# The order of the weight-part products, half-size weight buffers and side-by-side gate products in a two-layer decoder kernel

## The chip, the cores and the metric

The kernel runs on one core of one Trainium2 chip. The metric is the device time of one execution, in microseconds (us), taken as the median of several runs. Lower is better.

## The reference, cut to what matters

A small decoder with two layers works on 272 tokens (16 learned "meta" tokens and 256 input tokens) of width 2048, with 16 heads of 128.

```python
h = concat([meta, x])                        # 272 x 2048
# layer 0: attention with forget gates
a = rms_norm(h, norm_attn[0])
q, k, v, f_logit = split(a @ fox_w_in)       # 3 x 2048 columns, and 16 of f_logit
cum_logf = cumsum(log_sigmoid(f_logit + b_f))
h = h + forgetting_attention(q, k, v, cum_logf) @ fox_w_o
h = h + square(relu(rms_norm(h, norm_mlp[0]) @ w_up[0])) @ w_down[0]      # D_FF = 8192
# layer 1: stick-breaking attention over one shared K/V
k, v = split(rms_norm(h, kv_norm) @ w_kv)
q = rms_norm(h, norm_attn[1]) @ sb_w_q
h = h + stick_breaking_attention(q, k, v) @ sb_w_o
h = h + square(relu(rms_norm(h, norm_mlp[1]) @ w_up[1])) @ w_down[1]
return rms_norm(h, final_norm)[16:]          # the meta tokens are dropped
```

All is float32. Nearly the whole of the arithmetic is in the products with the weight matrices.

## The kernel before, in words

**Layout.** Activations lie feature-major: `hT` has 128 partitions, 16 chunks of features and 272 tokens. Layer 1 needs the meta tokens only for keys and values, so its queries, output projection and MLP run on 256 tokens; layer 0 and the keys and values of layer 1 run on 272.

**Split products.** A float32 product is made of products of the faster type `float32r`. Each weight block is split into a high part `whi` (ScalarE copies it into float32r, L205) and a low part `wlo` (VectorE subtracts the high part from the weights, L206). The activations are split in the same way, into `hi` and `lo`, which lie side by side in one tile (`both`). The product is high by high, high by low and low by high. In layer 0 these are three products of 272 columns (L228, L229, L230). In layer 1 the first two are one product of 512 columns, `whi` with `both` (L225), and the third is a product of 256 columns, `wlo` with `hi` (L226). Such a couple is called a pair. The two halves of a layer 1 bank are added when the bank is evacuated (`total`, L238 to L243: a ScalarE copy, a VectorE add).

**Groups.** `gemm_group` (L169 to L232) computes 512 output columns over all 2048 features. It runs four blocks `kb` of 512 features; a block has four chunks `kc` of 128. The 512 columns are four slices `m` of 128, each with a PSUM bank of its own (`acc`; the pool `pacc` has four banks, so the next group takes over the banks of this one as they are evacuated). A group thus has 64 (`kc`, `m`) steps: 192 products in layer 0, 64 pairs in layer 1. There are 96 groups in order: 12 of layer 0's queries, keys and values (Q, K, V for each of four sets of heads), 4 of its output projection, 32 of its MLP (four times 4 up and 4 down), then 4 of layer 1's queries, 8 of its keys and values, 4 of its output projection and 32 of its MLP.

**Weights.** One block is 1 MB, loaded by SyncE into a buffer `raw` (pool `wraw`, three buffers, L38) by one DMA (L193). Each half of a block (two chunks) is split into one `whi` and one `wlo` (pool `wspl`, three of each, L41). In the first group the DMAs are finer, 1, 2, 2 and 4 chunks by block, and `load_x` (L251) loads and splits the input between them.

**Order.** Inside a block the products are written half by half, and in each half bank by bank with two chunks each (L212); in the last block bank by bank with all four chunks (L216); in the first block of the first group chunk by chunk (L214). This written order isn't the one that runs: the program is built by a scheduler that simulates the engines in time and gives each engine a queue of its own; it may move a product past another whose data it expects later. At run time every engine works through its queue in order, and semaphores hold an instruction back until its data is there.

**Norms.** RMS norms are applied after the products: a group multiplies with the weights first, and the evacuation multiplies by `rstd`. `Norm.add` (L141) sums squares by chunk; `Norm.finish` (L150) makes a product with a matrix of 1/2048 (L153) into a bank `pms` of the pool `patt` and then a chain on VectorE and ScalarE. In the first up group of an MLP, `get_rstd` (L460) is called ahead of block 3; so is `get_rstd1` (L501) in the first query group of layer 1 (L514).

**Gates.** Group 1 is the first query group. Behind it come the gates (L281): 48 products of 272 columns with 16-column weights (L286, L287, L288), a VectorE multiplication by `rstd`, the bias, a logarithm of the sigmoid (ScalarE and VectorE), a cumulative sum over tokens (a scan on VectorE, L299), two transposes, and a trip through DRAM that spreads the sums over the partitions (`fk`, L358). The keys' group follows, and `decays` (L361, L364) are VectorE instructions behind the weight splits of its blocks.

**Start.** Seven products of a constant with itself (`idle`, L59 and L60) run on TensorE before the first data is there.

## Time and profile before

| | |
|---|---|
| Median of 3 runs | 2354.8 us (2354.66 to 2355.55) |
| The profiled run | 2355.27 us |
| Its span, first to last instruction | 2353.6 us |
| TensorE busy (PE) | 2339.7 us, 99% |
| VectorE busy (DVE) | 1343.7 us, 57% |
| ScalarE busy (ACT) | 1056.2 us, 45% |
| GpSimd busy (POOL) | 33.4 us, 1% |
| Weights and all else moved by DMA | 411.92 MB, 175 GB/s in the mean |
| Granted TensorE clock, mean over the span | 0.998 of full |

How to read it: one execution is recorded by the hardware's profiler. PE is TensorE's row of products, PEld its row of weight loads, which run beside the products. A product's recorded length holds its way through the array, and the next one starts before it ends; so what counts for the throughput is the distance from one start to the next, and not the length. "L225" is line 225 of the kernel. In a timeline, "x4" is four like instructions in a row, with the time from the first start to the last end. "[0.94 <-DVE ssq_a L148]" says that the engine stood idle for 0.94 us ahead of this instruction, and what it waited for. In a table of windows each row is a stretch of time, its length, and then for PE, PEld, DVE, ACT and POOL the busy time and the number of instructions, followed by the granted TensorE clock, the share of the DMA engines in use and GB/s. In a list of the costliest groups the columns are the busy time, the mean length in ns of one, and the idle time ahead of them with its releaser.

### The profile page before, as it was taken

The page shows a single profiled execution, that of the slowest core. Times are in us where ns is not written, and L with a number is a line of the kernel's source. Part 1 is how long each engine was busy: PE and PEld are TensorE (multiplying, and loading weights), DVE is VectorE, ACT ScalarE, POOL GpSimd, SP SyncE. Part 2 cuts the span into 40 slices and gives each one's busy share as a digit, 9 for nine tenths or more (in the row PEclk, how much of TensorE's full clock was granted, in tenths as well). Part 3 has the DMA queues.
Part 4 walks back from the last instruction along what each step waited for, and adds up shares of the span by engine and source line. Part 5 has one row for each costly group of instructions (what it writes and reads, how often), then busy time and mean ns, then how long its engine had stood idle before and what let it go on. Part 6 is the DMA issues. An engine that isn't in the chain of part 4 may idle for free.

```text
span 2353.6 us, 39103 instructions
## 1 busy us (share of the span) xinstructions
PE 2339.7 (99%) x16496; PEld 2207.5 (94%) x16496; DVE 1343.7 (57%) x1920; ACT 1056.2 (45%) x1471; POOL 33.4 (1%) x58
## 2 busy tenths in 40 slices
PE   9999999999999999999999999999999999999998
PEld 9999999999999999999998999988888888888887
DVE  7565555655454455455566555566555655655665
ACT  5434344544343344344445444445544543543543
POOL 1000000000000000000000000000000000000000
PEclk9999999999999999999999999999999999999999
DMA  6444444544555454545545444445545555455453
GB/s 231 157 157 171 171 162 162 179 176 168 178 177 179 171 188 162 186 172 179 180 162 196 162 145 143 146 175 179 193 178 186 196 179 197 174 187 196 178 197 125
DMA packets 61040, 411.92 MB, mean 175 GB/s; under 512 B 7089, under 2 KB 10049, under 8 KB 12097
## 3 DMA queue, kind: packets, MB, share of 16 engines
q1 hardware_dynamic: 58976, 406.27, 48.6%
q10 hardware_dynamic: 1888, 3.16, 0.4%
q8 instruction: 129, 2.11, 0.4%
q14 instruction: 47, 0.38, 0.0%
HBM read 407.29 MB, written 2.11 MB: 174 GB/s over the span
## 4 chain that ended last, share of the span: by engine, by line
PE 99%; DVE 0%; ACT 0%; DMA 0%; issue 0%; DVEq 0%; SPq 0%; ACTq 0%
PE acc L225 25%; PE acc L228 19%; PE acc L229 19%; PE acc L230 19%; PE acc L226 13%; PE ps L376 0%; PE pza L555 0%; PE pv L315 0%; PE po L438 0%; PE po L594 0%; PE pzb L556 0%; PE po L595 0%; PE po L439 0%; DMA g_sb<-gains 0%; ACT whi L205 0%; PE po L596 0%
## 5 line engine op out<-in xcount | busy, mean ns | idle before, releaser
L206 DVE TENSOR_TENSOR wlo<-raw,whi 128x1024 fp32r<-128x1024 f32 (+1 forms) x771 | 932.9, 1220 | 751.8 <-ACT whi L205 748.6
L205 ACT ACTIVATE whi<-raw 128x1024 fp32r<-128x1024 f32 (+1 forms) x771 | 803.2, 1054 | 1064.5 <-PE acc L229 669.8
L225 PE MATMUL acc<-x_m,whi 128*128 128x512 f32 x1024 | 343.2, 394 | 0.5 <-DVE relu L243 0.5
L225 PE MATMUL acc<-x_u,whi 128*128 128x512 f32 x1008 | 338.0, 394 | 0.0
L228 PE MATMUL acc<-x_u,whi 128*128 128x272 f32 (+1 forms) x1040 | 297.7, 289 | 0.0
L229 PE MATMUL acc<-x_u,whi 128*128 128x272 f32 (+1 forms) x1040 | 294.8, 286 | 0.0
L228 PE MATMUL acc<-x_m,whi 128*128 128x272 f32 x1024 | 293.4, 289 | 0.0
L229 PE MATMUL acc<-x_m,whi 128*128 128x272 f32 x1024 | 290.4, 286 | 0.0
L230 PE MATMUL acc<-x_u,wlo 128*128 128x272 f32 (+1 forms) x1040 | 285.2, 284 | 0.0
L230 PE MATMUL acc<-x_m,wlo 128*128 128x272 f32 x1024 | 280.7, 284 | 0.0
L226 PE MATMUL acc<-x_m,wlo 128*128 128x256 f32 x1024 | 252.7, 282 | 0.0
L226 PE MATMUL acc<-x_u,wlo 128*128 128x256 f32 x1008 | 247.6, 281 | 0.0
L228 PE MATMUL acc<-x_a,whi 128*128 128x272 f32 x768 | 222.6, 294 | 0.8 <-ACT x_a L130 0.8
L229 PE MATMUL acc<-x_a,whi 128*128 128x272 f32 x768 | 220.2, 291 | 0.0
L225 PEld LDWEIGHTS acc<-x_m,whi 128*128 128x128 f32 x1024 | 185.0, 188 | 30.3 <-DVE relu L243 0.9
L230 PE MATMUL acc<-x_a,wlo 128*128 128x272 f32 x768 | 211.2, 288 | 0.0
L226 PEld LDWEIGHTS acc<-x_m,wlo 128*128 128x128 f32 x1024 | 192.3, 188 | 19.6 <-DVE wlo L206 4.7
L225 PEld LDWEIGHTS acc<-x_u,whi 128*128 128x128 f32 x1008 | 182.4, 188 | 29.8
L226 PEld LDWEIGHTS acc<-x_u,wlo 128*128 128x128 f32 x1008 | 189.3, 188 | 15.8 <-DVE wlo L206 1.5
L228 PEld LDWEIGHTS acc<-x_u,whi 128*128 128x128 f32 x1040 | 195.5, 188 | 0.2
L229 PEld LDWEIGHTS acc<-x_u,whi 128*128 128x128 f32 x1040 | 195.1, 188 | 0.1
L228 PEld LDWEIGHTS acc<-x_m,whi 128*128 128x128 f32 x1024 | 192.5, 188 | 0.0
(249 smaller groups left out, 3601.3 us busy)
## 6 DMA issues: line engine op xcount, KB each, us to landing
raw<-w_up SPq DMA_DIRECT2D x128, 1024.0 KB, 4.8
raw<-w_dn SPq DMA_DIRECT2D x128, 1024.0 KB, 4.8
raw<-w_qkv SPq DMA_DIRECT2D x45, 1024.0 KB, 4.8
raw<-w_o SPq DMA_DIRECT2D x32, 1024.0 KB, 4.8
raw<-w_kv SPq DMA_DIRECT2D x32, 1024.0 KB, 4.8
raw<-w_q SPq DMA_DIRECT2D x16, 1024.0 KB, 4.9
fk<-f_dram ACTq DMA_DIRECT2D x4, 544.0 KB, 5.7
raw<-w_qkv SPq DMA_DIRECT2D x4, 512.0 KB, 8.2
```

The lines of the kernel that those rows point to most:

```text
L205: on_act = nc.scalar.activation(hp, src, AF.Copy)
L206: on_dve = nc.vector.tensor_tensor(out=lp, in0=src, in1=hp.bitcast(F32), op=ALU.subtract)
L225: nc.tensor.matmul(accs[m], wh, sp.both[:, k], start=first, stop=False)
L226: nc.tensor.matmul(accs[m][:, :n], wl, hi, start=False, stop=last)
L228: nc.tensor.matmul(accs[m][:, :n], wh, hi, start=first, stop=False)
L229: nc.tensor.matmul(accs[m][:, :n], wh, lo, start=False, stop=False)
L230: nc.tensor.matmul(accs[m][:, :n], wl, hi, start=False, stop=last)
```

## The change

- **Order of products.** In the first and the last block of a group the products now run bank by bank over all four chunks, in the two middle blocks half by half over all four banks. Within such a stretch all products of the high weight part come first and all of the low part after them: in layer 1 four and four in blocks 0 and 3, eight and eight in blocks 1 and 2. In layer 0 the three products of a step stay together.
- **Queued as written.** `gemm_matmul` ties each product of a group to the one before it with a dependence that needs no semaphore, so that the scheduler keeps the written order; the first group isn't tied.
- **Half-size buffers.** A `raw` buffer now holds half a block (two chunks), there are four of them, and each half has a DMA of its own (one DMA for each chunk in the first two blocks of the first group). There are four `whi` and four `wlo` buffers.
- **Gates.** High and low weights of the gates lie side by side in one tile of 32 columns, and 32 products, with `xa.hi` and `xa.lo`, are issued straight behind group 1 and ahead of the norm. After the norm their two halves are multiplied by `rstd`, copied to SBUF and added by one more product with two identities one above the other (`both`). Group 1's banks are copied to `qT` by ScalarE without `rstd`, and VectorE multiplies `qT` afterwards.
- **Norms.** `get_rstd` and `get_rstd1` are called ahead of block 2 instead of block 3.
- **Start.** Nine idle products instead of seven.

```diff
@@ -35,10 +35,10 @@
     nc = tc.nc
 
     const = ctx.enter_context(tc.tile_pool(name="const", bufs=1))
-    wraw = ctx.enter_context(tc.tile_pool(name="wraw", bufs=3))
+    wraw = ctx.enter_context(tc.tile_pool(name="wraw", bufs=4))
 
     align = ctx.enter_context(tc.tile_pool(name="align", bufs=1))
-    wspl = ctx.enter_context(tc.tile_pool(name="wspl", bufs=3))
+    wspl = ctx.enter_context(tc.tile_pool(name="wspl", bufs=4))
     xs = ctx.enter_context(tc.tile_pool(name="xs", bufs=2))
     tmp = ctx.enter_context(tc.tile_pool(name="tmp", bufs=2))
     att = ctx.enter_context(tc.tile_pool(name="att", bufs=2))
@@ -56,7 +56,7 @@
     nc.vector.memset(mean_w, 1.0 / D)
 
     idle = patt.tile([P, 512], F32, tag="patt", name="idle")
-    for _ in range(7):
+    for _ in range(9):
         nc.tensor.matmul(idle[:, :P], mean_w, mean_w, start=True, stop=True)
     ident = const.tile([P, P], F32, name="ident")
     make_identity(nc, ident)
@@ -165,6 +165,15 @@
             return r
 
     uid = [0]
+    queued, pinned = [], [False]
+
+    def gemm_matmul(*args, **kw):
+
+        ins = nc.tensor.matmul(*args, **kw).ins
+        if queued and pinned[0]:
+            tc.add_manual_dep(ins, queued[0].name, mybir.DependencyInfo(mybir.DependencyClass.NoSync,
+                                                                        mybir.DependencyReason.DATA))
+        queued[:] = [ins]
 
     def gemm_group(wblk, sp, t0, evac, before={}, after={}, load_x=None, pairs=False, apart=()):
 
@@ -177,21 +186,20 @@
         accs = [pacc.tile([P, 512], F32, tag="acc", name=f"acc_{u}_{m}") for m in range(4)]
         n = T - t0
         for kb in range(4):
-            raw = wraw.tile([P, 4, 512], F32, tag="raw", name=f"raw_{u}_{kb}")
             src_w = wblk[kb].rearrange("p (k c) -> p k c", k=4)
             if kb in before:
                 before[kb]()
-            piece = 4 if load_x is None else (1, 2, 2, 4)[kb]
+            piece = 1 if load_x is not None and kb < 2 else 2
+            raws = [wraw.tile([P, 2, 512], F32, tag="raw", name=f"raw_{u}_{kb}_{hf}") for hf in range(2)]
             for k0 in range(0, 4, piece):
                 if load_x is not None:
                     load_x(range(4 * kb + k0, 4 * kb + k0 + piece))
                 if load_x is not None and kb == k0 == 0:
 
                     for c0 in (0, 256):
-                        nc.scalar.dma_start(raw[:, 0, c0:c0 + 256], src_w[:, 0, c0:c0 + 256])
+                        nc.scalar.dma_start(raws[0][:, 0, c0:c0 + 256], src_w[:, 0, c0:c0 + 256])
                 else:
-                    nc.sync.dma_start(raw[:, k0:k0 + piece], src_w[:, k0:k0 + piece])
-            piece = min(piece, 2)
+                    nc.sync.dma_start(raws[k0 // 2][:, k0 % 2:k0 % 2 + piece], src_w[:, k0:k0 + piece])
             parts = []
             for hf in range(2):
                 whi = wspl.tile([P, 2, 512], F32R, tag="whi", name=f"whi_{u}_{kb}_{hf}")
@@ -200,7 +208,7 @@
                 if load_x is not None and kb == hf == 0:
                     boxes[:1] = [(0, 1, 0, 256), (0, 1, 256, 512)]
                 for o, no, c0, c1 in boxes:
-                    src = raw[:, 2 * hf + o:2 * hf + o + no, c0:c1]
+                    src = raws[hf][:, o:o + no, c0:c1]
                     hp, lp = whi[:, o:o + no, c0:c1], wlo[:, o:o + no, c0:c1]
                     on_act = nc.scalar.activation(hp, src, AF.Copy)
                     on_dve = nc.vector.tensor_tensor(out=lp, in0=src, in1=hp.bitcast(F32), op=ALU.subtract)
@@ -208,28 +216,36 @@
             if kb in after:
                 with tc.issue_after(on_act.ins), tc.issue_after(on_dve.ins):
                     after[kb]()
-            order = [(kc, m) for hf in range(2) for m in range(4) for kc in range(2 * hf, 2 * hf + 2)]
+
+
             if load_x is not None and kb == 0:
-                order = [(kc, m) for kc in range(4) for m in range(4)]
-            if kb == 3:
-                order = [(kc, m) for m in range(4) for kc in range(4)]
-            for kc, m in order:
-                whi, wlo = parts[kc // 2]
-                k = 4 * kb + kc
-                wh = whi[:, kc % 2, m * P:(m + 1) * P]
-                wl = wlo[:, kc % 2, m * P:(m + 1) * P]
-                first = kb == 0 and kc == 0
-                last = kb == 3 and kc == 3
-                hi, lo = sp.hi[:, k], sp.lo[:, k]
-                if pairs and m not in apart:
-                    nc.tensor.matmul(accs[m], wh, sp.both[:, k], start=first, stop=False)
-                    nc.tensor.matmul(accs[m][:, :n], wl, hi, start=False, stop=last)
-                else:
-                    nc.tensor.matmul(accs[m][:, :n], wh, hi, start=first, stop=False)
-                    nc.tensor.matmul(accs[m][:, :n], wh, lo, start=False, stop=False)
-                    nc.tensor.matmul(accs[m][:, :n], wl, hi, start=False, stop=last)
-                if last:
-                    evac(m, [accs[m][:, :n]] + ([accs[m][:, n:]] if pairs and m not in apart else []))
+                runs = [([kc], range(4)) for kc in range(4)]
+            elif kb in (0, 3):
+                runs = [(range(4), [m]) for m in range(4)]
+            else:
+                runs = [(range(2 * hf, 2 * hf + 2), range(4)) for hf in range(2)]
+            pinned[0] = load_x is None
+            for kcs, ms in runs:
+                paired = [m for m in ms if pairs and m not in apart]
+                single = [m for m in ms if m not in paired]
+                for kc in kcs:
+                    for m in paired:
+                        gemm_matmul(accs[m], parts[kc // 2][0][:, kc % 2, m * P:(m + 1) * P], sp.both[:, 4 * kb + kc],
+                                    start=kb == kc == 0, stop=False)
+                for kc in kcs:
+                    for m in paired:
+                        gemm_matmul(accs[m][:, :n], parts[kc // 2][1][:, kc % 2, m * P:(m + 1) * P],
+                                    sp.hi[:, 4 * kb + kc], start=False, stop=kb == kc == 3)
+                for m in single:
+                    for kc in kcs:
+                        wh, wl = (w[:, kc % 2, m * P:(m + 1) * P] for w in parts[kc // 2])
+                        hi, lo = sp.hi[:, 4 * kb + kc], sp.lo[:, 4 * kb + kc]
+                        gemm_matmul(accs[m][:, :n], wh, hi, start=kb == kc == 0, stop=False)
+                        gemm_matmul(accs[m][:, :n], wh, lo, start=False, stop=False)
+                        gemm_matmul(accs[m][:, :n], wl, hi, start=False, stop=kb == kc == 3)
+                if kb == 3:
+                    for m in ms:
+                        evac(m, [accs[m][:, :n]] + ([accs[m][:, n:]] if m in paired else []))
 
     def residual_add(c, acc, t0):
         for a in acc:
@@ -261,8 +277,6 @@
             box["wf"] = load_gates()
         for c in range(4 * kb, 4 * kb + 4):
             norm.add(c)
-        if kb == 3:
-            box["rstd"] = norm.finish()
 
     fq_sb = const.tile([P, 2, NC], F32, name="fq_sb")
     fqm_sb = const.tile([64, 4], F32, name="fqm_sb")
@@ -270,27 +284,33 @@
 
     def load_gates():
         nc.scalar.dma_start(bf_sb, b_f)
+
         wf_sb = att.tile([P, NC, NC], F32, tag="v_sb", name="wf_sb")
-        wf_hi = att.tile([P, NC, NC], F32R, tag="pm_sb", bufs=1, name="wf_hi")
-        wf_lo = att.tile([P, NC, NC], F32R, tag="v_sb", name="wf_lo")
+        wf = att.tile([P, NC, 2 * NC], F32R, tag="v_sb", name="wf")
         nc.scalar.dma_start(wf_sb, w_f)
-        nc.scalar.activation(wf_hi, wf_sb, AF.Copy)
-        nc.vector.tensor_tensor(out=wf_lo, in0=wf_sb, in1=wf_hi.bitcast(F32), op=ALU.subtract)
-        return wf_hi, wf_lo
+        nc.scalar.activation(wf[:, :, :NC], wf_sb, AF.Copy)
+        nc.vector.tensor_tensor(out=wf[:, :, NC:], in0=wf_sb, in1=wf[:, :, :NC].bitcast(F32), op=ALU.subtract)
+        both = att.tile([P, P], F32, tag="pk", name="both")[:2 * NC, :NC]
+        nc.vector.tensor_tensor(out=both, in0=ident[:2 * NC, :NC], in1=ident[:2 * NC, NC:2 * NC], op=ALU.add)
+        return wf, both
+
+    def gate_products():
+        wf, _ = box["wf"]
+        pf = box["pf"] = patt.tile([P, 512], F32, tag="patt", name="pf")
+        for k in range(NC):
+            nc.tensor.matmul(pf[:2 * NC, :T], wf[:, k, :], xa.hi[:, k], start=k == 0, stop=False)
+            nc.tensor.matmul(pf[:2 * NC, :T], wf[:, k, :], xa.lo[:, k], start=False, stop=k == NC - 1)
 
     def forget_gates(rstd):
 
-        wf_hi, wf_lo = box["wf"]
-        pf = patt.tile([P, 512], F32, tag="patt", name="pf")
-        for k in range(NC):
-            nc.tensor.matmul(pf[:NC, :T], wf_hi[:, k, :], xa.hi[:, k], start=k == 0, stop=False)
-            nc.tensor.matmul(pf[:NC, :T], wf_hi[:, k, :], xa.lo[:, k], start=False, stop=False)
-            nc.tensor.matmul(pf[:NC, :T], wf_lo[:, k, :], xa.hi[:, k], start=False, stop=k == NC - 1)
+        parts = tmp.tile([P, T], F32, tag="relu", name="parts")[:2 * NC]
+        nc.vector.tensor_tensor(out=parts, in0=box["pf"][:2 * NC, :T], in1=rstd[:2 * NC, :], op=ALU.mult)
+        pf = patt.tile([P, 512], F32, tag="patt", name="pf_sum")
+        nc.tensor.matmul(pf[:NC, :T], box["wf"][1], parts, start=True, stop=True)
         fx = tmp.tile([P, T], F32, tag="relu", name="fx")[:NC]
         fe = tmp.tile([P, T], F32, tag="u2", name="fe")[:NC]
         fc = tmp.tile([P, T], F32, tag="relu", name="fc")[:NC]
-        nc.vector.tensor_tensor(out=fx, in0=pf[:NC, :T], in1=rstd[:NC, :], op=ALU.mult)
-        nc.vector.tensor_scalar(fx, fx, bf_sb, None, op0=ALU.add)
+        nc.vector.tensor_scalar(fx, pf[:NC, :T], bf_sb, None, op0=ALU.add)
         nc.scalar.activation(fe, fx, AF.Abs)
         nc.scalar.activation(fe, fe, AF.Exp, scale=-1.0)
         nc.scalar.activation(fe, fe, AF.Ln, bias=1.0)
@@ -350,7 +370,13 @@
             nc.vector.tensor_tensor(out=t[:, m, :], in0=acc[0], in1=box["rstd"], op=ALU.mult)
 
         if g == 0:
-            gemm_group(w_qkv0[0], xa, 0, evac_q, after={kb: (lambda kb=kb: first_norm(kb)) for kb in range(4)}, load_x=load_x)
+
+            gemm_group(w_qkv0[0], xa, 0, lambda m, acc, qT=qT: nc.scalar.copy(qT[:, m, :], acc[0]),
+                       after={kb: (lambda kb=kb: first_norm(kb)) for kb in range(4)}, load_x=load_x)
+            gate_products()
+            box["rstd"] = norm.finish()
+            for m in range(4):
+                evac_q(m, [qT[:, m, :]])
             forget_gates(box["rstd"])
         else:
             gemm_group(w_qkv0[3 * g], xa, 0, evac_q)
@@ -473,7 +499,7 @@
                     nc.scalar.activation(u.hi[:, c], u2[:, t0:], AF.Copy)
                     nc.vector.tensor_tensor(out=u.lo[:, c], in0=u2[:, t0:], in1=u.hi[:, c].bitcast(F32),
                                             op=ALU.subtract)
-                gemm_group(w_up[layer, f, g], xm, t0, evac, {3: get_rstd} if f == g == 0 else {},
+                gemm_group(w_up[layer, f, g], xm, t0, evac, {2: get_rstd} if f == g == 0 else {},
                            pairs=t0 == M)
             for g in range(4):
                 def evac(m, acc, g=g):
@@ -511,7 +537,7 @@
             for c in ([4 * kb + g - 1] if g < 3 else [4 * kb + 2, 4 * kb + 3]):
                 split_chunk(xc, G_KV, c)
 
-        gemm_group(w_q1[g], xq, M, evac_q1, {3: get_rstd1} if g == 0 else {},
+        gemm_group(w_q1[g], xq, M, evac_q1, {2: get_rstd1} if g == 0 else {},
                    after={kb: (lambda kb=kb: split_c(kb)) for kb in range(4)} if g else {}, pairs=True)
 
     ao = Split("o1", M)
```

## The prediction, made before the result was known

> **What bounds the kernel now.** I read the page first, for the engine that sets the end.
>
> ```profile
> span 2353.6 us, 39103 instructions
> ...
> PE 2339.7 (99%) x16496; PEld 2207.5 (94%) x16496; DVE 1343.7 (57%) x1920; ACT 1056.2 (45%) x1471; POOL 33.4 (1%) x58
> ...
> PE 99%; DVE 0%; ACT 0%; DMA 0%; issue 0%; DVEq 0%; SPq 0%; ACTq 0%
> ```
>
> TensorE is busy for 99% of the span and is 99% of the chain that ended last. So only three things can pay: fewer products, a shorter spacing from one product to the next, and the few holes in its row. The profiled run took 2355.27 us, its span 2353.6; the median of the three timed runs, 2354.8, is 0.5 below that run.
>
> Next, busy time by stretch, each stretch cut at the first product of a group: a layer 0 group; four groups of layer 1 that each follow a down group (three down, one up), then four that each follow an up group (three up, one down); the first query group and the first up group of layer 1; the stretch between group 1 and group 2; and the clock's change at the start (columns: length, then busy and count for each engine).
>
> ```profile
> 484.59:508.48 23.89, 23.89 (x194) 23.89 (x193) 12.79 (x16) 11.16 (x17) 0.00 (x0) 1.00 0.49 177
> 1731.33:1821.03 89.70, 89.70 (x514) 78.38 (x513) 49.05 (x64) 33.75 (x35) 0.00 (x0) 1.00 0.52 188
> 1821.03:1911.59 90.56, 90.56 (x515) 77.94 (x513) 56.05 (x82) 47.40 (x79) 0.00 (x0) 1.00 0.51 186
> 1201.39:1225.40 24.01, 23.07 (x132) 19.87 (x130) 15.39 (x22) 13.07 (x21) 0.00 (x0) 1.00 0.49 175
> 1617.19:1640.72 23.53, 23.00 (x132) 19.85 (x130) 16.98 (x28) 13.49 (x22) 0.00 (x0) 1.00 0.50 179
> 31.33:38.97 7.64, 6.70 (x53) 4.96 (x52) 5.63 (x13) 1.92 (x3) 0.24 (x1) 1.00 0.43 139
> 8.00:9.00 1.00, 1.00 (x6) 1.00 (x6) 1.00 (x3) 0.81 (x2) 0.00 (x0) 1.00 0.84 262
> 9.00:10.00 1.00, 1.00 (x10) 1.00 (x9) 0.60 (x3) 0.73 (x2) 0.00 (x0) 1.00 1.03 413
> ```
>
> A layer 0 group is 192 products in 23.89 us, 124.4 ns each, without a hole; its order hardly changes and I give it nothing. A layer 1 group is 64 pairs: a product of the high weight part with 512 columns (L225, "H" below) and one of the low part with 256 (L226, "L"). Behind a down group it takes 89.70 / 4 = 22.43 us, 350.4 ns a pair; behind an up group 22.64, 0.21 more; the first query group takes 1.58 more, the first up group 1.10 more.
>
> The waits of TensorE and of its weight loads name the holes (total us, times, longest):
>
> ```profile
> PE acc L225 <- DVE qT L243: 0.9, 1, 0.9
> PE pms_a L153 <- DVE ssq_a L148: 0.9, 1, 0.9
> PE acc L225 <- DVE relu L243: 0.5, 1, 0.5
> PEld acc L226 <- DVE wlo L206: 7.0, 18, 0.4
> ```
>
> **The change, part by part.**
>
> *Low part late, 18 times.* One of them, in the timeline of TensorE (start, length):
>
> ```profile
> 1829.47 1.10 PE L225 MATMUL acc<-x_m,whi 128*128 128x512 f32 x4
> 1830.51 0.39 PE L226 MATMUL acc<-x_m,wlo 128*128 128x256 f32 x1
> 1830.74 0.40 PE L225 MATMUL acc<-x_m,whi 128*128 128x512 f32 x1
> ```
>
> Four H take 1.04 us and the L after them 0.23; without a wait these are 0.92 and 0.12 (below), so a wait costs 0.23, as the windows say with 0.21. With four split buffers instead of three, and the low part asked for after four or eight H instead of at once, it should be there: 18 x 0.215 = **-3.9** us. Bounds: -3.9, and 0 if the splits come late anyway.
>
> *Norms one block earlier.* In the first query group and the first up group the bank of the next group's first products is freed late, behind the norm's chain on VectorE. Issuing the norm in block 2 instead of 3 moves that chain a quarter group, 5.6 us, ahead; the sums of squares that it reads end with the group before, more than a block earlier. The norm's own product stays, about 0.4 us. So 1.58 + 1.10 - 0.8 = 1.9 by the windows and 0.9 + 0.5 = 1.4 by the waits: **-1.6**.
>
> *Series of one part.* This is the largest and least certain term. Inside one down group:
>
> ```profile
> 1776.53 0.40 PE L225 MATMUL acc<-x_u,whi 128*128 128x512 f32 x1
> ...
> 1777.59 0.86 PE L225 MATMUL acc<-x_u,whi 128*128 128x512 f32 x3
> ...
> 1779.33 0.40 PE L226 MATMUL acc<-x_u,wlo 128*128 128x256 f32 x2
> 1779.57 0.39 PE L225 MATMUL acc<-x_u,whi 128*128 128x512 f32 x1
> ...
> 1780.39 1.09 PE L225 MATMUL acc<-x_u,whi 128*128 128x512 f32 x4
> 1781.31 0.28 PE L226 MATMUL acc<-x_u,wlo 128*128 128x256 f32 x1
> ```
>
> From 1776.53 to 1777.59, H and L strictly alternate, three pairs: 353 ns a pair. Four H in a row take 0.92 us, 230 ns each. Two L in a row take 0.24 at 1779.33 and nearly as much elsewhere, 118 to 120 each. The 350.4 of a whole group is then a mixture, since the present order holds alternation and short runs. The new order is four H and four L by bank in blocks 0 and 3, eight and eight in blocks 1 and 2. I take 230 + 118 = 348, so -2.4 ns a pair; layer 1 has 2544 pairs (queries, output, 16 up and 16 down groups, less the few kept apart): **-6.1** us. No run of L longer than two stands in the trace. The ends: L at half of 230, 115, gives 345 and -13.7; the alternating 353 for every pair gives +6.6.
>
> The Trainium skill, "TensorE: Matmul & The Clock Gate", section "Back-to-back issue gap", has N/2.4 + 2.5 ns for a product of N columns: 215.8 + 109.2 = 325 a pair in any order. The trace's 350.4 says that this is not the whole cost, and the 353 beside it that order is felt; by the rule the term would be zero, which is a rival below.
>
> *Gates.* The rows between group 1 and group 2:
>
> ```profile
> 32.42 0.73 PE L153 MATMUL pms_a<-ssq_a,mean_w 128*128 128x272 f32 x2 [0.94 <-DVE ssq_a L148]
> 32.79 0.49 PE L286 MATMUL pf<-x_a,wf_hi 128*16 128x272 f32 x1
> 33.11 0.29 PE L287 MATMUL pf<-x_a,wf_hi 128*16 128x272 f32 x1
> ...
> 38.97 0.28 PE L228 MATMUL acc<-x_a,whi 128*128 128x272 f32 x1
> ```
>
> 47 products in 5.86 us, 125 ns each. High and low gate weights side by side need 32 products, 4.0 us; the 32 columns instead of 16 cost nothing, as a 128-column load hides beneath the same product all through layer 0. The norm's product (0.37 and some 0.2 of turning round) moves into group 2, and the sum of the halves is a second such: 1.1 together. The wait of 0.94 goes, since gate products fill it. 7.64 - 4.0 - 1.1 = **-2.5**. Evacuating group 1 by four ScalarE copies frees its banks without the norm; rescaling them is four VectorE instructions as before.
>
> *What that delays.* The gate sum now stands in block 2 of group 2, the transposes in block 3 instead of 1. Behind them come the round trip through DRAM and the decays, on VectorE ahead of weight splits of group 3:
>
> ```profile
> 42.26 0.71 DVE L299 TENSOR_TENSOR_SCAN fc<-fx,fe 16x272 f32<-16x272 f32 x1
> 52.83 2.17 DVE L364 SCALAR_TENSOR_TENSOR s<-fk,fq_sb,maskA 128x144 f32<-128x144 f32 x6 [1.57 <-DMA fk<-f_dram]
> ```
>
> From the scan's end (42.97) to the decays are 9.9 us. Some 10 us later than now, they end about where group 3 wants its last key bank and its second block. VectorE already waits 1.57 here; as a TensorE wait that is 0 to 1.6: **+0.7**.
>
> *Start.*
>
> ```profile
> 1.12 3.35 PE L60 MATMUL idle<-mean_w 128*128 128x128 f32 x14 [1.12 <-DVE mean_w L56]
> 5.26 1.28 PE L228 MATMUL acc<-x_a,whi 128*128 128x272 f32 x4 [0.79 <-ACT x_a L130]
> 12.99 1.23 DVE L206 TENSOR_TENSOR wlo<-raw,whi 128x1024 fp32r<-128x1024 f32 x1 [0.26 <-ACT whi L205]
> ```
>
> Up to 9 us TensorE starts 6 products a us, after that 10: it is granted half speed until then. Two more idle products (four records of 0.21) close most of the hole of 0.79, so full speed may come up to 3.4 us earlier: 16 products x 0.1 = 1.6 at best. But data limits: block 1's low part ends at 14.22, where TensorE waits already. The finer pieces in block 1 let some of the gain through: **-1.0** (0 to -1.6).
>
> *Half-size buffers and the pinned queue.*
>
> ```profile
> L206 DVE TENSOR_TENSOR wlo<-raw,whi 128x1024 fp32r<-128x1024 f32 x766 | 929.8, 1224 | 749.8 <-ACT whi L205 746.6 <-PE acc L226 2.5
> L205 ACT ACTIVATE whi<-raw 128x1024 fp32r<-128x1024 f32 x766 | 800.5, 1057 | 1061.2 <-PE acc L229 669.8 <-PE acc L225 384.1 <-issue 4.0
> L242 ACT COPY relu<-acc 128x256 f32<-128x256 f32 x64 | 23.1, 363 | 41.5 <-PE acc L226 40.1
> L243 DVE TENSOR_TENSOR relu<-acc,relu 128x256 f32<-128x256 f32 x64 | 27.0, 423 | 27.9 <-ACT relu L242 27.4
> raw<-w_up SPq DMA_DIRECT2D x128, 1024.0 KB, 4.8
> L193 SPq DMA_DIRECT2D raw<-w_up x128: 327/328/328, 418.6 to 2228.6; - x128
> ```
>
> SyncE issues twice the weight loads, some 770 x 0.33 = 250 us, and has little else to do. TensorE eats a half block in 22.43 / 8 = 2.8 us and a raw buffer returns after four: 11.2, less the split (1.06 + 1.22) and at most 4.8 for landing (2.4 if it went by size) leaves 4 us. No cost.
>
> TensorE can no longer step past a late buffer. The tightest place I see is bank 3 in a group that follows an up group in layer 1. Count from the up group's end, E. Bank 2 is done at E - 1.4. In the changed program's queue ScalarE then has its copy, a square and a copy (some 0.4 each), the two splits of the next block 1 and bank 3's copy: 0.36 + 0.8 + 2.1 + 0.36 = 3.6, E + 2.2; VectorE's add follows a split, about E + 3.9. Block 0 now goes bank by bank, so bank 3 is wanted after three quarters of it, E + 4.2. Slack 0.3. I put **+1.0** for small waits of this kind behind the 16 up groups.
>
> Sum: -3.9 - 1.6 - 6.1 - 2.5 + 0.7 - 1.0 + 1.0 = **-13.4**. 2355.3 - 13.4 = 2341.9 for a run like the profiled one, 2341.4 beside the median.
>
> **Rivals.** *Order is not felt* (chance 0.15): the mixture already costs what the series will, the term of 6.1 is nothing: 2347.5. For it, three H at 1777.59 and couples of L are no faster than the mean; against it, alternation's 353. *Holes stay* (0.07): the splits are late by other waits, 3.9 and 1.6 stay: 2347. *Strict order bites* (0.08), the slower side: bank 3's chain comes 2.3 us later than counted, by one more split on each engine, and TensorE stands 2.0 us behind each of 16 up groups, +32 for my +1.0: 2372. It decides for slower from about 1.2 us a group. Against it: ScalarE is busy 47.40 of 90.56 us there. That the series aren't formed is excluded: the built queue has them.
>
> **How the numbers follow.** My case has 0.70, 2341.4, by its own bounds 2333 to 2350. A measurement tells 0.2%, 4.7 us, from no change. The range 2332 to 2352 takes in the first two rivals and leaves out the slower one and the far ends. Faster: nearly all of 0.70, two thirds of 0.22, less a little for late data: 0.80. Same 0.12, slower 0.08.
>
> **What would show it.** Groups of layer 1 at 22.3 us instead of 22.43, behind up groups too; no weight load waiting for L206's result; 5 us between groups 1 and 2; ten products a us before 9. Wrong: H and L in series at 353 or more a pair, or waits of acc products for VectorE behind up groups.

## The result, and the profile after

The changed kernel takes 2332.21 us (median of 5 runs, 2332.05 to 2332.84) against 2354.97 for the kernel before in the same session (5 runs): a ratio of 0.9903, 95% interval 0.9889 to 0.9916. That is 22.8 us less; the prediction said 13.4 less, and the low end of its range, 2332.0, lies 0.2 below the measured time.

The page of the profiled execution (2332.09 us):

```profile
span 2330.3 us, 39954 instructions
...
PE 2319.3 (100%) x16486; PEld 2200.1 (94%) x16486; DVE 1350.6 (58%) x1923; ACT 1064.8 (46%) x1477; POOL 38.9 (2%) x58
...
PE 99%; DVE 0%; ACT 0%; issue 0%; DVEq 0%; ACTq 0%
```

TensorE is still the bound, with nearly as many products as before (16486 against 16496), but its busy time is 20.4 us shorter: mostly the same products, closer together. Windows, cut at the first product of a group, show where. In order: a layer 0 group; three down groups and an up group of layer 1; three up groups and a down group; the first query group; the first up group; and groups 1 and 2.

```profile
480.66:504.56 23.90, 23.90 (x195) 23.90 (x193) 12.75 (x16) 11.37 (x17) 0.00 (x0) 1.00 0.53 177
1720.06:1808.43 88.37, 88.37 (x514) 77.66 (x513) 51.49 (x65) 35.00 (x39) 0.00 (x0) 1.00 0.60 191
1808.43:1896.80 88.37, 88.37 (x514) 77.67 (x513) 56.47 (x80) 47.44 (x75) 0.00 (x0) 1.00 0.58 191
1197.46:1220.11 22.65, 22.65 (x133) 19.86 (x131) 16.09 (x25) 12.09 (x19) 0.00 (x0) 1.00 0.57 186
1609.15:1631.68 22.53, 22.53 (x132) 19.80 (x131) 16.49 (x27) 12.50 (x21) 0.00 (x0) 1.00 0.57 188
...
5.12:33.81 28.69, 28.67 (x225) 27.76 (x225) 26.80 (x48) 25.43 (x52) 1.00 (x4) 1.00 0.90 320
33.81:60.56 26.75, 26.75 (x209) 25.78 (x207) 14.68 (x25) 10.29 (x13) 2.64 (x1) 1.00 0.45 155
```

Groups 1 and 2 of the kernel before, cut in the same way:

```profile
5.26:38.97 33.71, 32.77 (x243) 30.77 (x244) 28.97 (x54) 23.80 (x47) 1.29 (x4) 1.00 0.81 298
38.97:64.49 25.52, 25.52 (x204) 25.23 (x203) 14.92 (x26) 9.41 (x11) 0.00 (x0) 1.00 0.41 146
```

Layer 0 is unchanged. A layer 1 group takes 88.37 / 4 = 22.09 us, 345.2 ns a pair, and it does so behind up groups as well as behind down groups; only the query groups behind the first take 22.17. Group 1 with the gates is 5.0 us shorter and group 2 is 1.2 longer. Where the kernel before had 18 waits for `wlo`, the list of the waits of weight loads now begins with this row, and no row of it names `wlo` or L214, the line of the subtraction:

```profile
PEld pr_fin L665 <- DVE fin L659: 1.4, 1, 1.4
```

The timeline of TensorE shows the series (start, length; all products are at L172 now, `whi` with 512 columns is H, `wlo` with 256 is L):

```profile
1720.06 1.07 PE L172 MATMUL acc<-x_u,whi 128*128 128x512 f32 x4
1720.97 0.63 PE L172 MATMUL acc<-x_u,wlo 128*128 128x256 f32 x4
1721.44 1.09 PE L172 MATMUL acc<-x_u,whi 128*128 128x512 f32 x4
1722.37 0.62 PE L172 MATMUL acc<-x_u,wlo 128*128 128x256 f32 x4
1722.82 1.07 PE L172 MATMUL acc<-x_u,whi 128*128 128x512 f32 x4
```

From start to start: four H in 0.91 us, four L in 0.47 (118 ns each), four H in 0.93, four L in 0.45 (113 each), and again 0.92. There are two kinds of L series, and the faster one, 113 ns, was no part of the prediction's 118. The trace of the kernel before held it already: of its 540 couples of L, 93 take 113 to 114 ns each (one stands at 1729.2).

Summed over groups by their first products: the start, the gates and what follows to the end of group 3 give -3.9 (of which the gates -2.4); the late low parts -3.8; the first query and first up group -1.7 beyond what their neighbours gained; the spacing in 40 layer 1 groups -13.2; the last group -0.4 more; keys and values of layer 1 -0.2. Together -23.2, as the profiled executions differ (2355.27 and 2332.09).

### The profile page after: what moved, and what is told of

It is laid out like the page before. It is cut to its first block, busy times and chain, and to the rows that moved or that the text cites. A ratio compares the mean times of both kernels' runs of the same rounds, so it can differ in the third digit from the quotient of the medians.

```text
span 2330.3 us, 39954 instructions
## 1 busy us (share of the span) xinstructions
PE 2319.3 (100%) x16486; PEld 2200.1 (94%) x16486; DVE 1350.6 (58%) x1923; ACT 1064.8 (46%) x1477; POOL 38.9 (2%) x58
## 4 chain that ended last, share of the span: by engine, by line
PE 99%; DVE 0%; ACT 0%; issue 0%; DVEq 0%; ACTq 0%
PE acc L172 96%; PE ps L402 0%; PE pza L581 0%; PE pv L335 0%; PE po L464 0%; PE po L620 0%; PE idle L60 0%; PE pzb L582 0%; PE po L621 0%; PE po L465 0%; PE po L622 0%; DVE ob L676 0%; PE pf L301 0%; PE pf L302 0%; PE pta L597 0%; PE pta L596 0%
## 5 line engine op out<-in xcount | busy, mean ns | idle before, releaser
L214 DVE TENSOR_TENSOR wlo<-raw,whi 128x1024 fp32r<-128x1024 f32 (+1 forms) x773 | 931.7, 1217 | 752.6 <-ACT whi L213 751.7
L172 PE MATMUL acc<-x_u,whi 128*128 128x272 f32 (+2 forms) x3088 | 650.8, 322 | 0.0
L172 PE MATMUL acc<-x_m,whi 128*128 128x272 f32 (+1 forms) x3072 | 649.2, 323 | 0.0
L172 PEld LDWEIGHTS acc<-x_u,whi 128*128 128x128 f32 x3088 | 497.4, 188 | 26.3
L172 PEld LDWEIGHTS acc<-x_m,whi 128*128 128x128 f32 x3072 | 495.5, 188 | 26.9
L172 PE MATMUL acc<-x_u,wlo 128*128 128x272 f32 (+1 forms) x2048 | 441.7, 280 | 0.0
L172 PE MATMUL acc<-x_m,wlo 128*128 128x272 f32 (+1 forms) x2048 | 439.4, 280 | 0.0
L172 PE MATMUL acc<-x_a,whi 128*128 128x272 f32 (+1 forms) x1792 | 363.0, 307 | 0.0
L172 PEld LDWEIGHTS acc<-x_u,wlo 128*128 128x128 f32 x2048 | 339.5, 188 | 15.9
L172 PEld LDWEIGHTS acc<-x_m,wlo 128*128 128x128 f32 x2048 | 338.5, 188 | 16.1
L172 PEld LDWEIGHTS acc<-x_a,whi 128*128 128x128 f32 x1792 | 283.5, 188 | 9.3 <-issue 0.7
L172 PE MATMUL acc<-x_a,wlo 128*128 128x272 f32 (+1 forms) x1024 | 252.9, 284 | 0.0
L172 PE MATMUL acc<-x_kv,whi 128*128 128x272 f32 x1024 | 195.8, 289 | 0.0
L172 PEld LDWEIGHTS acc<-x_a,wlo 128*128 128x128 f32 x1024 | 179.3, 188 | 4.7 <-issue 0.5
L172 PE MATMUL acc<-x_o,whi 128*128 128x272 f32 (+1 forms) x768 | 163.1, 323 | 0.0
L172 PEld LDWEIGHTS acc<-x_kv,whi 128*128 128x128 f32 x1024 | 159.9, 188 | 0.4
L172 PE MATMUL acc<-x_kv,wlo 128*128 128x272 f32 x512 | 145.9, 285 | 0.0
L172 PEld LDWEIGHTS acc<-x_o,whi 128*128 128x128 f32 x768 | 124.0, 188 | 6.7
L172 PE MATMUL acc<-x_o,wlo 128*128 128x272 f32 (+1 forms) x512 | 110.8, 282 | 0.0
L172 PEld LDWEIGHTS acc<-x_kv,wlo 128*128 128x128 f32 x512 | 96.2, 188 | 0.1
```

Of the source, the lines that this page charges most:

```text
L172: ins = nc.tensor.matmul(*args, **kw).ins
L214: on_dve = nc.vector.tensor_tensor(out=lp, in0=src, in1=hp.bitcast(F32), op=ALU.subtract)
```

## The experiments

Each run is compared with the kernel before on the same chip (medians 2355.2 to 2355.7). The changed kernel was timed in the first session only, beside 2354.97, so a difference to it of less than 1 us isn't told apart. Group 2 begins between 33.81 and 35.96 us in profiles that have the changed kernel's first group in common, so differences of 1 to 2 us are read from group lengths. Group lengths are from first product to first product.

**Theory and rivals.** Theory A: the order of the products alone sets their spacing; buffers, gates and norm each remove a wait of their own, and the parts add up. Rival B: the half-size loads and buffers make the spacing. Rival C: an order that can't step aside needs the additional split buffers. Later two more theories on the series: P, a phase; L, their length.

**1. Order only.** The kernel before with the new order, tied, and nothing else:

```diff
+    def gemm_matmul(*args, **kw):
...
-            order = [(kc, m) for hf in range(2) for m in range(4) for kc in range(2 * hf, 2 * hf + 2)]
...
+            elif kb in (0, 3):
+                runs = [(range(4), [m]) for m in range(4)]
+            else:
+                runs = [(range(2 * hf, 2 * hf + 2), range(4)) for hf in range(2)]
```

> The kernel before with one part of the change: the new order of the products, tied as written; 1 MB buffers (three), three split buffers, old gates, old place of the norm, seven idle products. Theory A, the spacing follows from the order alone: layer 1 groups behind a down group at 22.09 us as in the changed kernel (22.43 before), -0.34 x 40 = -13.5. If the order also cures the late low parts (they are asked for later), another -3.8: 2337 to 2338 us; if it doesn't, 2341 to 2342. Rival B, the shorter spacing comes from the half-size loads and buffers: groups stay at 22.43 and the time at 2351 or more. Rival C, an order that can't step aside needs the fourth split buffer: waits of TensorE for whi or wlo in many groups, slower than 2342, possibly than before.

Measured: 2414.04 us, ratio 1.025 (1.0232 to 1.0267). The order by itself makes the kernel 59 us slower: rival C. A layer 0 group takes 24.8 to 24.9 us instead of 23.89, a layer 1 MLP group 22.8 to 22.9. The waits of its weight loads:

```profile
PEld acc L172 <- DVE wlo L215: 58.2, 78, 1.0
PEld acc L172 <- ACT whi L214: 12.8, 42, 2.1
```

One such wait on three engines, as a group begins at 647.89 (ScalarE, VectorE, TensorE):

```profile
647.22 2.01 ACT L214 ACTIVATE whi<-raw 128x1024 fp32r<-128x1024 f32 x2 [4.17 <-PE acc L172]
```

```profile
648.45 2.35 DVE L215 TENSOR_TENSOR wlo<-raw,whi 128x1024 fp32r<-128x1024 f32 x2
```

```profile
648.64 0.41 PE L172 MATMUL acc<-x_m,whi 128*128 128x272 f32 x2
649.72 0.40 PE L172 MATMUL acc<-x_m,wlo 128*128 128x272 f32 x1 [0.67 <-DVE wlo L215]
```

ScalarE waited 4.17 us for TensorE to finish with a split buffer and could split only at 647.22, since the products of the last block, written bank by bank, use both halves of their block to the end. The first block of the next group, bank by bank too, wants the low part of its second half in its third step already. VectorE begins it at 648.45, and TensorE can go on at 649.72. Within series the spacing is that of the changed kernel (H at 226, 229 and 232 in turn, then L at 113 or 118), so theory A stands for the spacing and falls on the sum.

**2. Three split buffers.** The changed kernel with `wspl` at `bufs=3`, one number.

> The changed kernel with three split buffers of each part instead of four, all else as changed (half-size weight buffers, tied order, new gates, early norm). Theory A: the tied order asks for the second half of a block while the first is in use, and with three split buffers that half is late; the waits of the order-only run come back, 0.95 us in a layer 0 group and 0.8 in a layer 1 group: 44 x 0.95 + 40 x 0.8 = +74, 2395 to 2410 us, in any case slower than before. Rival: it is the half-size weight buffers that free the order (a half is loaded and split on its own): 2332 to 2338.

Measured: 2414.13 us, ratio 1.0248 (1.0233 to 1.0264), the time of the order-only run; 24.86 us a layer 0 group. Its weight loads wait as there:

```profile
PEld acc L172 <- DVE wlo L214: 59.5, 80, 1.0
PEld acc L172 <- ACT whi L213: 11.9, 42, 1.2
```

So the fourth split buffer is worth 82 us in this kernel (the sum in the expectation, +74, was of the right size), and the half-size weight buffers, which this run has, don't make up for it.

**3. Buffers only.** The kernel before with the four half-size weight buffers, their loads and the four split buffers, in the old order.

```diff
-    wraw = ctx.enter_context(tc.tile_pool(name="wraw", bufs=3))
+    wraw = ctx.enter_context(tc.tile_pool(name="wraw", bufs=4))
-    wspl = ctx.enter_context(tc.tile_pool(name="wspl", bufs=3))
+    wspl = ctx.enter_context(tc.tile_pool(name="wspl", bufs=4))
```

> The kernel before with one part of the change: four half-size weight buffers with a load each (one per chunk in the first two blocks of the first group) and four split buffers; the scheduler orders the products as it likes, old gates, old norm, seven idle products. Theory A: nothing of the spacing, groups behind down groups at 22.43; the 18 late low parts may go (-3.9), as the prediction had it, and the first group gains up to 1 from its finer pieces: 2350 to 2355 us. Rival B: groups at 22.09, 2338 or less. If the late low parts stay, it was the order that cured them.

Measured: 2356.47 us, ratio 1.0005 (0.9996 to 1.0014), no difference. Groups behind down groups keep the old spacing, 90.01 / 4 = 22.50 us (22.43 before), and those behind up groups are now as fast, 89.83 / 4 = 22.46 (22.64 before):

```profile
1733.23:1823.24 90.01, 90.01 (x514) 78.53 (x513) 50.33 (x65) 35.12 (x39) 0.00 (x0) 1.00 0.57 187
1823.24:1913.07 89.83, 89.83 (x515) 78.54 (x514) 55.19 (x80) 46.92 (x75) 0.00 (x0) 1.00 0.55 188
```

Rival B falls, and the late low parts do go. But a new wait takes their place, between group 1 and group 2:

```profile
35.70 1.27 PE L153 MATMUL pms_a<-ssq_a,mean_w 128*128 128x272 f32 x2 [5.36 <-DVE ssq_a L148]
```

The norm's product waits 5.36 us for the sum of squares, where it waited 0.94. VectorE's row shows why: with a fourth split buffer the scheduler lets it split further ahead, and the last three sums of squares stand behind a split that itself waits for ScalarE.

```profile
32.98 1.22 DVE L205 TENSOR_TENSOR wlo<-raw,whi 128x1024 fp32r<-128x1024 f32 x1 [1.69 <-ACT whi L204]
34.12 1.53 DVE L148 TENSOR_TENSOR ssq_a<-ssq_a,sq_a 128x272 f32<-128x272 f32 x3
```

Behind the wait the gate products are spaced 0.23 us up to 39.27 and 0.125 from 39.44 on; the granted clock from 35.70 to 39.40 is 0.51. Group 1 takes 4.8 us more than in the kernel before (38.50 instead of 33.70), and this eats what the low parts and the first query and up groups gain.

**4. Gates of before.** The changed kernel with the 48 gate products behind the norm, and group 1 evacuated through it.

```diff
-            gate_products()
-            box["rstd"] = norm.finish()
-            for m in range(4):
-                evac_q(m, [qT[:, m, :]])
             forget_gates(box["rstd"])
```

> The changed kernel with the gates of before: 48 products behind the norm, group 1 evacuated through the norm; all else as changed. The prediction's sum: +2.5, 2334.7 us. Theory I (interaction): with more buffers the scheduler puts weight splits ahead of the sums of squares, as in the buffers-only run, where TensorE waited 5.4 us for the norm's sum instead of 0.94; the gate products of the change cover that wait, and taking them away costs 2.4 + 4.5 = +7: 2339.

Measured: 2341.91 us, ratio 0.9942 (0.9926 to 0.9959), 9.7 above the changed kernel. The same wait is back:

```profile
35.81 0.82 PE L153 MATMUL pms_a<-ssq_a,mean_w 128*128 128x272 f32 x1 [5.38 <-DVE ssq_a L148]
```

In the changed kernel gate products run in its place, and neither the norm's product nor the sum of the halves waits:

```profile
27.84 0.29 PE L301 MATMUL pf<-x_a,wf 128*32 128x272 f32 x1
...
33.69 0.29 PE L302 MATMUL pf<-x_a,wf 128*32 128x272 f32 x1
...
36.80 0.62 PE L153 MATMUL pms_a<-ssq_a,mean_w 128*128 128x272 f32 x2
46.55 0.63 PE L309 MATMUL pf_sum<-parts,both 32*16 32x272 f32 x2
```

Theory I holds: beside the other parts the gates are worth 9.7 us, not 2.5 nor the 7 that theory I expected. What theory I left out are slow products behind the wait:

```profile
35.81:40.40 4.59, 4.59 (x18) 2.92 (x19) 2.19 (x6) 0.86 (x2) 0.00 (x0) 0.50 0.33 115
```

At a granted clock of 0.50 the gate products are spaced 0.23 us instead of 0.125 until 40.28, some 2.1 us in all with the norm's products. Groups 1 and 2 give 9.1 of the 9.7: 5.4 of wait, 16 x 0.125 = 2.0 of products, the 2.1, and small differences that come to -0.4.

**5. Alternate.** The changed kernel with each series written high, low, high, low.

> The changed kernel with the products of a series alternated: high, low, high, low, still tied as written, all else as changed. Theory A: strict alternation costs 353.3 ns a pair as it did in short stretches of the kernel before, 22.61 us a group, 0.52 x 40 = +20.8 over the changed kernel: 2353 us. Rival B (buffers, loads, or a queue that no longer steps aside make the spacing): groups stay near 22.1, time within 3 us of 2332. In between (350.4 a pair, 2345) would say that series count but that alternation isn't the far end.

Measured: 2352.72 us (ratio 0.9989, 0.998 to 0.9999), 20.5 above the changed kernel. That is more than the 13.2 which the order gained, since strict alternation is slower than the mixture of the kernel before. Four groups, and the timeline:

```profile
1726.21:1816.66 90.45, 90.45 (x514) 78.88 (x513) 50.68 (x65) 35.07 (x39) 0.00 (x0) 1.00 0.54 187
```

```profile
1726.21 0.40 PE L172 MATMUL acc<-x_u,whi 128*128 128x512 f32 x1
1726.45 0.28 PE L172 MATMUL acc<-x_u,wlo 128*128 128x256 f32 x1
1726.57 0.39 PE L172 MATMUL acc<-x_u,whi 128*128 128x512 f32 x1
```

90.45 / 4 = 22.61 us a group, 353.3 ns a pair, as expected. With the same products, buffers, banks and tie, only the order within a series differs: the spacing is a matter of order.

**6. Series of three.** In layer 1 the steps of a block are cut into series of 3, 3, 3, 3, 4 (even blocks) and 4, 3, 3, 3, 3 (odd).

> The changed kernel with other lengths of series in layer 1: three high then three low throughout, with one series of four at the end of even blocks and at the start of odd ones. Theory P (phase): in the changed kernel's trace high products in a row are spaced 226, 229, 232 ns over and over, and a series of low ones takes 113.3 each if it follows the third of them and about 118 otherwise. Series of three always end on the third: (687 + 340) / 3 = 342.3 a pair; with the two fours in each two blocks 343.2, against 345.2: 2544 x -2.0 = -5.1, 2327 us. Rival L (length): what helps is the length of a series (the eights of the changed kernel take 344.7 a pair, the fours 345.9), so threes give 346.5 or more: 2335 or slower.

Measured: 2330.82 us (2330.53 to 2330.98), 1.4 below the changed kernel where P said 5. In the MLP groups P is right, 21.96 us. In the query and output groups it isn't, 22.39; these six groups lose 1.6 against the changed kernel, the start and the last group 0.6 each. A series of each kind, from an MLP group and from an output group:

```profile
1721.80 0.85 PE L172 MATMUL acc<-x_u,whi 128*128 128x512 f32 x3
1722.49 0.50 PE L172 MATMUL acc<-x_u,wlo 128*128 128x256 f32 x3
1722.83 0.85 PE L172 MATMUL acc<-x_u,whi 128*128 128x512 f32 x3
1723.51 0.50 PE L172 MATMUL acc<-x_u,wlo 128*128 128x256 f32 x3
...
1566.58 0.86 PE L172 MATMUL acc<-x_o,whi 128*128 128x512 f32 x3
1567.28 0.52 PE L172 MATMUL acc<-x_o,wlo 128*128 128x256 f32 x3
```

In the first kind three H take 0.69 us (226, 229 and 232 ns) and three L 0.34; in the second 0.70 (233, 236, 229), and their L 120, 118 and 117. Either repeats itself for as long as the series stay threes: 342.3 or 351 ns a pair. Series of three don't choose the phase, they keep it.

**7. Threes in step.** The same, with the fours at the other ends in the query and output groups.

> The run with series of three, with the fours at the start of even blocks and at the end of odd ones in the query and output groups of layer 1 (49 to 52, 61 to 64), where the low products stayed at 118; the MLP groups as in that run. Theory P (phase): a four moves the series from one phase to the other; these groups came in with the wrong one, so the swapped places keep them in the right one: groups 50 to 52 and 62 to 64 at 21.96 instead of 22.39, 2330.8 - 6 x 0.43 = 2328.2 us. Rival: the slower series hang on the operands (other tiles of x), not on the phase: 22.39 stays, 2330.8.

Measured: 2330.52 us (2329.93 to 2330.93), not told from run 6. Groups 50 and 51 do go from 22.39 to 21.96: a series of four moves one phase into the other, as P says, on the same operands. Group 52 stays at 22.42. But the output groups take 22.39 again. They come out of group 61 in a third phase (H at 229, 232, 226, L at 118), and the two series of four where group 62 begins turn it into the slow one (H at 233, 236, 229): after 61's interruptions the phase isn't known beforehand. The mechanism is right, the gain was missed: 2330.5 where 2328.2 was expected.

**8. Many orders.** Other orders in eight groups each (the last in seven).

> The changed kernel with other orders in the two MLPs, a different one for each eight groups, everything still computed. Layer 0, groups 17 to 24: in each series all high-by-high, then all high-by-low, then all low-by-high; 25 to 32: high-by-low first in each step; 33 to 40: high-by-high and high-by-low in turn, then all low-by-high; 41 to 48: low-by-high and high-by-high in turn, then all high-by-low. Now a step takes 126.5 + 126 + 121 ns, 23.89 us a group. If series of one part help there as in layer 1, the first order takes 121 each and 23.2 us a group; if the 121 comes from the change of part, it takes 126 and 24.2. Layer 1, groups 65 to 72: series of sixteen; 73 to 80: six, six, four and four, six, six; 81 to 88: two; 89 to 95: twelve, four and four, twelve. Now 22.09 us. Theory P (phase of three): six and twelve as threes, 21.96; sixteen and two 22.0 to 22.3. Theory L (length): sixteen fastest, two slowest, near alternation's 22.6.

Measured (2374.89 us, one run): a layer 0 group by part, a six-six-four group, a group of twos, and one of sixteens behind an up group:

```profile
554.54:578.78 24.24, 24.24 (x194) 24.24 (x193) 11.32 (x12) 8.26 (x9) 0.00 (x0) 1.00 0.52 174
...
1930.20:1952.16 21.96, 21.96 (x130) 19.31 (x129) 12.65 (x17) 8.26 (x9) 0.00 (x0) 1.00 0.57 191
2018.16:2040.24 22.08, 22.08 (x130) 19.44 (x129) 14.10 (x21) 12.34 (x21) 0.00 (x0) 1.00 0.59 190
1640.43:1666.92 26.49, 23.88 (x128) 20.65 (x129) 13.82 (x21) 12.15 (x20) 0.00 (x0) 0.94 0.47 159
```

Twos take what the changed kernel's fours and eights take, 22.08: theory L falls. Sixes are as fast as threes behind down groups (21.96) and fall into the other phase or wait behind up groups (22.73). Sixteens and twelves wait, against theory P's 21.96 for the twelves (24.2 behind up groups and 22.9 behind down groups; 21.96 only in the first of them, behind a group of twos): their low products come last, the banks finish close together, and the next group finds none free (26.49 us, of which TensorE is idle for 2.61, waiting for the evacuation at L300). In layer 0 a series of one part is worse, 24.24, and no order beats 23.89.

**9. Layer 0 orders.** Eight more orders of the three products, four groups each.

> The changed kernel with eight other orders of the three products of a step in the MLP of layer 0, four groups each (17 to 48), everything still computed; HH, HL and LH are high weights by high x, high by low, low by high. In turn: HH HL LH LH HL HH over two steps; LH HL HH; HH LH HL; LH HH HL; by part over three steps; by part over two; HH HL HH HL LH LH; LH HL in turn over four steps, then HH. Now 23.89 us a group (127, 126, 121 ns in turn). In the run with high-by-high and high-by-low in turn, stretches of 125 and 121.5 stood, 123.3 in the mean: an order that holds them throughout gives 23.7. If instead the spacing of 272 columns is the same whatever the order, but for the phase, all eight lie between 23.7 and 24.3, and the present one is among the best. An order at 121 throughout would be 23.2.

Measured (2335.85 us, one run): 23.89 us a group for six of the eight, 24.13 for threes by part and 24.00 for twos by part. Layer 0 has nothing to gain from order; leaving it as it was is right.

**10. Two big weight buffers.** Two 1 MB buffers with one load each, in the place of four halves.

> The changed kernel with two 1 MB weight buffers and a load each instead of four of half that size: the same SBUF, four split buffers, all else as changed. Theory A (four split buffers decide, the size of the loads doesn't): a 1 MB load lands in 4.8 us, its splits take 2.3 more, so two buffers deliver a block each 4 us or so, against the 5.5 that TensorE takes: 2332 to 2334 us. Rival: halves are needed, since a big buffer comes free only after its second half is split: waits of TensorE for whi in most groups, 2340 or more.

Measured: 2333.03 us (2332.66 to 2333.49), not told from the changed kernel, with its group lengths throughout but for group 1 (0.9 more) and the last (0.4 more). Halving the loads is worth nothing that stands out. Both kernels hold 2 MB of weight buffers where the kernel before held 3; that this makes the room for the fourth split buffer is likely, but no run tried three big buffers beside four split buffers.

**11. Seven idle products, late norm.** Two small edits undone.

> The changed kernel with two small parts undone, which touch different groups: seven idle products instead of nine (groups 1 and 2), and the norms of the first query group and of the first up group ahead of block 3 again (groups 49, 50, 65, 66). The prediction's terms: +1.6 for the norms, group 49 at 23.7 and group 65 at 23.2 us instead of 22.64 and 22.53; +0.5 to +1.6 for the idle products: 2334.3 to 2335.4 us. Rival for the norms: in the buffers-only run, with the norm at its old place, these groups took 0.6 and 0.5 more than their neighbours, not 1.5 and 0.9; so it is the fourth split buffer that took the wait away, and the place of the norm is worth 0.2 at most. Rival for the idle products: the start before the first weights is set by data, the group 1 lengths of the runs so far (28.7 to 29.6 with nine) differ by as much: below 0.5. Both rivals: 2332.2 to 2333.

Measured: 2336.41 us (2334.22 to 2337.38). The median lies above all that was expected. Of the norms: group 49 takes 22.57 (22.64 changed), so its early norm is worth nothing; behind group 65 one wait comes back, group 66 at 22.96 instead of 22.09:

```profile
1199.57:1222.14 22.57, 22.57 (x132) 19.80 (x131) 15.19 (x23) 12.10 (x19) 0.00 (x0) 1.00 0.59 188
1633.72:1656.68 22.96, 22.34 (x130) 19.48 (x129) 15.15 (x23) 13.21 (x25) 0.00 (x0) 1.00 0.57 183
```

Of the start nothing is settled: group 2 begins 2.1 us later than in the changed kernel, but in the two other profiles of that session, with nine idle products, it begins as late (35.96 in run 7, 35.60 in run 9). The rest of the difference lies there and at the very end: from the last group's first product to the start of the program's last product there are 27.24 us in the changed kernel, 28.01 here, 27.23 and 28.01 in runs 7 and 6. The last eight products, the same in all, are spaced 0.11 us where it is short and 0.21 where it is long.

**12. Untied.** The changed kernel without the tie.

> The changed kernel without the tie between products (the scheduler may move them again), all else as changed. In the built queue of 30 layer 1 MLP groups the high products then still stand in fours (227 times) and eights (90), with a few twos, sixes and tens, since the written order has them so and four split buffers leave little reason to step aside. Theory A (the written series give the spacing, the tie only keeps them): layer 1 groups at 22.1 to 22.2 us, 2332 to 2336 us. Rival: the tie is what holds the spacing; without it the scheduler's moves bring back the mixture, 22.4 a group, 2345.

Measured: 2334.03 us (2333.71 to 2334.21), 1.8 above the changed kernel. Groups take 22.09 behind down groups and 22.19 behind up groups. The written series do nearly all; the tie adds the last tenth.

## Why the prediction came out as it did

The direction, the bound and most of the terms were right; the gain was 1.7 times the one forecast. The time lies inside the stated range by 0.2 us, but 0.8 below the bounds that the prediction gave its own case, 2333 to 2350: the range held by luck, while the size of its main term failed.

- **Series of one part, -6.1: mis-sized, measured -13.2.** The forecast took 230 + 118 = 348 ns a pair and named 345 as the far end; 345.2 was measured. The H were right (229 to 230). The L were taken at 118; half of the series run at 113, and the couples at 113 in the trace before were left out when "118 to 120" was read from it. This term explains 7 of the 9 us that the forecast lacked. The spacing rule that the prediction weighed isn't borne out. The Trainium skill, "TensorE: Matmul & The Clock Gate", section "Back-to-back issue gap", gives N/2.4 + 2.5 ns as the gap of an isolated product and says that for a stream it is too long at 512 columns; the estimate of 325 ns a pair from it, in any order, was the prediction's. Here it is too short, 229 to 230 ns a 512-column product against its 215.8, and order counts: pairs at 342, 345, 351 and 353 ns were measured.
- **Low part late, -3.9: measured -3.8**, and by the fourth split buffer, as said: it goes in the buffers-only run too.
- **Norms, -1.6: measured -1.7, for a cause that is half wrong.** Run 11 shows that the earlier norm is worth 0.9 behind the first up group and nothing in the first query group. There the other parts took the wait away: group 49 takes 24.02 us before, 23.02 with the buffers only (run 3).
- **Gates, -2.5: measured -2.4** against the kernel before: the stretch of 7.64 us became 32 products in 4.0 us, and group 2 took 1.2 more. But this sum goes against a schedule that no longer exists. Beside the new buffers the old gates would have cost 9.7 us (run 4), the slow products behind the wait included.
- **Decays delayed, +0.7: measured +0.05.** Group 3 takes 28.02 us instead of 27.97.
- **Start, -1.0: about -1.5, cause open.** The spacing bears the prediction out where it spoke of half speed, though the clock column says 1.00 there: products start 0.23 us apart up to 9.05 us before, and 0.13 apart from 6.21 on after the change. But run 11, with seven idle products, comes to 0.13 at 6.40, so the two additional ones aren't shown to be the cause. Where the window of the kernel before counts 6 products, those of the changed kernel and of run 11 count 10 (a count includes products that are in flight as the window opens; the prediction read it as starts, of which 0.23 and 0.13 us give some 4.4 and 8 a us):

```profile
8.00:9.00 1.00, 1.00 (x10) 1.00 (x9) 1.00 (x3) 1.00 (x3) 0.00 (x0) 1.00 0.93 319
8.00:9.00 1.00, 1.00 (x10) 1.00 (x9) 1.00 (x3) 0.59 (x2) 0.00 (x0) 1.00 0.89 271
```

  The gain is also no larger than the 2.2 us by which group 2's begin differs between profiles with the same first group.
- **Waits of the strict queue, +1.0 and "no cost" for the buffers: measured nothing**, since groups behind up groups take the same 22.09. The place was misjudged, though: the strict order does bite, by 82 us, if one split buffer is taken away (run 2), and not at bank 3's evacuation, where the slower rival put it.

Three of the parts can't be had one by one: the order alone loses 59 us, the buffers alone gain nothing, and together they need the gates to cover the norm's wait. The prediction added each part to the kernel before; that its smaller terms came out near is partly luck.

## What to carry to other kernels

Where TensorE is busy for 99% of the time, look at the distance between starts, product by product: on the same work the order in which two sizes of product follow each other made up to 3% of a group (342 to 353 ns a pair). Tie an order only when the buffers let it run, and test the parts together with what they need, since the same order shortened the spacing by 13 us with four split buffers and made the kernel 59 us slower with three. When a queue is given more room to run ahead, ask which chain it will now run ahead of.

## What the runs showed that was not expected

- **Spacing has a phase.** H products in a row are spaced 226, 229, 232 ns over and over (the first behind slow L up to 238); L products that follow the 232 take 113 each, others 117 to 120. What sets the phase is open.
- **A hole can cost twice.** A wait of 2.61 us in run 8 is followed by three H at 231 to 337 ns and eight at 427 instead of 229: ten products in 3.48 us, at a mean granted clock of 0.61. The waits of 5.4 us in runs 3 and 4 are followed by slow products too, one of 1.85 us in run 1 (at 14.11) as well, and in run 2 one of 1.02 us with one of 0.74 behind it (at 55.68 and 56.94). No length of the hole decides it alone: behind one of 2.96 us in run 8 (at 1720.71) the H are spaced 225 to 236 ns from the second on, and the granted clock is 1.00.

```profile
1666.92 5.30 PE L172 MATMUL acc<-x_m,whi 128*128 128x512 f32 x15 [2.61 <-DVE relu L300]
```

```profile
1666.92:1670.40 3.48, 3.48 (x10) 2.74 (x11) 2.69 (x8) 2.12 (x7) 0.00 (x0) 0.61 0.76 268
1720.71:1724.20 3.49, 3.06 (x12) 2.10 (x12) 2.70 (x8) 2.13 (x7) 0.00 (x0) 1.00 0.77 261
```
